# Forming the last product of a decoder block from seven quarter products instead of eight, with the sums of the weights' quarters kept in DRAM

## The chip, the cores and the metric

The kernel runs on one core of a Trainium2 chip. The metric is device time in microseconds (us) of one execution. Runs of the kernel before took 837.92 us (median of 3, 837.61 to 838.16).

Names used below: TensorE (PE) does the matmuls, and its weight loads (PEld) overlap them; VectorE (DVE) and GpSimd (POOL) do elementwise work, ScalarE (ACT) casts and activations; SyncE (SP) issues the DMA transfers, one after the other in the order written. PSUM has eight banks of 128 x 512 floats, in which the matmuls accumulate.

## The reference

A decoder block with 512 tokens, width 1024 and one layer: two token mixers side by side, merged by gates, then a SwiGLU channel mixer and a final norm. The change touches the last two lines:

```python
h = rmsnorm(x, norm1_g); z = h @ w_in + b_in
...
x = x + m @ w_mix_out
h = rmsnorm(x, norm2_g)
x = x + (silu(h @ ffn_w1) * (h @ ffn_w3)) @ ffn_w2     # ffn width 2816 = 22 x 128
return rmsnorm(x, norm_f_g)
```

All is float32. The product with `ffn_w2` is 512 x 2816 times 2816 x 1024.

## The kernel before

Every large product is done in three terms. An operand `v` is split into `h`, a cast to TensorE's reduced float32 form, and `l = v - h`; a product is then `xh.wh + xh.wl + xl.wh`, three matmuls for each 128 x 128 by 128 x 512 block. The cast is made on ACT (line 108, `split_to`), the difference on the engine that the caller names (line 104, `sub`): POOL or DVE.

Weights stream through a list of chunks (`wchunk`, line 121). A chunk is loaded by SP into one of four raw tiles of 128 x 1024 (pool `raws`, 512 KB, line 128), then split into one of five tiles that hold both halves (pool `hls`, line 135). `weights(key)` (line 150) emits loads and splits up to four chunks beyond the one asked for. The tile framework orders the instructions of each engine and picks free buffers; each engine then works strictly in its order, and an instruction that waits holds up those behind it.

Long-lived tiles of 128 x 512 come from a pool of 69 (`longt`), short-lived ones from a pool of 5 (`shortt`). PSUM is a pool of six banks (`bank`) and one of two (`bank2`).

The parts that the change touches, in order of time:

- *Mixing product* (`mix_rows`, line 679). For each of four row tiles `t` of 128 tokens the residual `x2[t]` (two tiles of 128 x 512) gets the product added by DVE (line 683), is normed and kept in SBUF to the end of the kernel.
- *FFN stage, called f below* (lines 704 to 719). For each of the 22 chunks `j` of the FFN width, 48 matmuls make `p1` and `p3` (hidden x tokens, each 128 x 512) from the chunks `f1_j` and `f3_j`. `ffn_out` (line 698) applies silu on ACT, multiplies on DVE and splits the result into `g[j]`. The difference of a split is POOL's for `f1_j` and DVE's for `f3_j` (lines 216 and 217). Chunks go in the order 0, 1, 2, ...
- *Output stage, called o below* (lines 721 to 751). All eight PSUM banks hold the result, four row tiles by two halves. For each `k` of the 22 chunks of `ffn_w2`, 24 matmuls add to the banks; the last four `k` (`LAST`) are left to the end and done row tile by row tile. Behind each row tile stand the addition of the residual (line 737), squares on ACT with a running sum (lines 311 and 315), the root (line 316), its reciprocal (line 317), two scalings (lines 748 and 749) and two stores of 256 KB (line 751).

Of the kernel before, what the change touches and what calls it, by code (L numbers as in the profile page):

```python
# [25 lines left out]
NT = T // P  # L26
ND = D // P
NR = DR // P
NF = DF // P
# [46 lines left out]
def tile_block(ctx, tc, a, out):  # L76
    nc = tc.nc
    pool = lambda name, bufs, **k: ctx.enter_context(tc.tile_pool(name=name, bufs=bufs, **k))
    consts = pool("consts", 1)
    raws = pool("raws", RAW)  # L80
# [16 lines left out]

    def bank2(name):
        return psum2.tile([P, T], F32, tag="cv", name=name)

    vec, act, pe, pool_e = nc.vector, nc.scalar, nc.tensor, nc.gpsimd

    def sub(eng, o, x, y):
        eng.tensor_tensor(out=o, in0=x, in1=y, op=ALU.subtract)  # L104

    def split_to(h, l, full, eng, copy=act.copy):

        copy(h, full)  # L108
# [12 lines left out]
    def wchunk(key, src, kt, cols, where="hl", lo=pool_e, after=None):  # L121
        chunks.append((key, src, kt, cols, where, lo, after))
# [86 lines left out]
    LAST = 4  # L209
# [8 lines left out]
    w2 = a["ffn_w2"][0].rearrange("(k p) (o n) -> p k o n", p=P, o=1)  # L218
    for k in range(NF):
        wchunk(f"f2_{k}", w2[:, k, :, :], 1, D, lo=vec if k % 2 else pool_e)  # L220

# [7 lines left out]
    for name, n in ROWS:  # L229
# [4 lines left out]
        while done < n:  # L234
            m = min(n - done, P - row_at(at + done)[1])
# [70 lines left out]
    def rstd_of(halves, junk, between=None):  # L306

        i = n_stats[0]
        n_stats[0] += 1
        ss, r = stats[:, i, :2], stats[:, i, 2:3]  # L310
        act.activation(junk[0], halves[0], AF.Square, accum_out=ss[:, 0:1])
        vec.tensor_scalar(out=ss[:, 0:1], in0=ss[:, 0:1], scalar1=1.0 / D, scalar2=EPS, op0=ALU.mult, op1=ALU.add)
        if between:
            between()
        act.activation(junk[1], halves[1], AF.Square, accum_out=ss[:, 1:2])  # L315
        act.activation(r, ss[:, 1:2], AF.Sqrt, scale=1.0 / D, bias=ss[:, 0:1])
        vec.reciprocal(r, r)
        return r

    def turn_half(name, rows, gname, dest, hf, bk):  # L320

        cs = slice(hf * 256, hf * 256 + 256)
        for c in range(ND):
            ps = bk[c % len(bk)](f"{name}{hf}{c}")
            for t in range(2):
                src = rows[2 * hf + t][c // 4][:, (c % 4) * P : (c % 4 + 1) * P]
                pe.transpose(ps[:, t * P : (t + 1) * P], src, ident)  # L327
            g = pc(gname, c)
            h, l = (v[:, cs] for v in dest[c])
            act.activation(h, ps[:, :256], AF.Copy, scale=g)  # L330
            vec.scalar_tensor_tensor(out=l, in0=ps[:, :256], scalar=g, in1=h.bitcast(F32), op0=ALU.mult, op1=ALU.subtract)  # L331

    def parts_of(pair_tiles, cs=slice(0, T)):
        return [(h[:, cs], l[:, cs]) for h, l in pair_tiles]
# [9 lines left out]
    HALVES = [slice(0, 256), slice(256, 512)]  # L344
    EARLY = 2
# [42 lines left out]
    ab, e, s, s2, po, c4 = (sm[:, i, :] for i in range(6))  # L388
# [210 lines left out]
    y = []  # L599
# [28 lines left out]
    for j in range(8):  # L628
        ws = w_tiles(f"lo{j}_0", 5) + w_tiles(f"lo{j}_1", 5)
# [19 lines left out]
    def token_banks(name):  # L649
        return [[(bank if t < 3 else bank2)(f"{name}{t}{h}") for h in range(2)] for t in range(NT)]  # L650

    def token_mm(po_, n_k, k, x_, w_, t, h):
        xh, xl = (v[:, t * P : (t + 1) * P] for v in x_[k])
        wh, wl = w_[h]
        for i, (l_, r_) in enumerate(((xh, wh), (xh, wl), (xl, wh))):
            pe.matmul(po_[t][h], l_, r_, start=k == 0 and i == 0, stop=k == n_k - 1 and i == 2)  # L656
# [13 lines left out]
    for k in range(8 - LAST):  # L670
        w_ = w_halves(f"mx{k}")
# [21 lines left out]
    mix_rows(3)  # L693


    g = []

    def ffn_out(j, p1, p3):
        s_ = shortt(f"si{j}")
        act.activation(s_, p1, AF.Silu)  # L700
        vec.tensor_tensor(out=s_, in0=s_, in1=p3, op=ALU.mult)  # L701
        g.append(split(f"gg{j}", s_, vec))

    wf = [(w_tiles(f"f1_{j}", ND), w_tiles(f"f3_{j}", ND)) for j in range(EARLY)]
    pf = [(bank(f"f1_{j}"), bank(f"f3_{j}")) for j in range(EARLY)]
    for hf in range(2):
        if hf:
            turn_half("th", xs, "norm2_g", h2p, 1, [bank2])
        for j in range(EARLY):
            for w_, p_ in zip(wf[j], pf[j]):  # L710
                mm3(p_[:, HALVES[hf]], w_, parts_of(h2p, HALVES[hf]))
    h2 = parts_of(h2p)
    for j in range(EARLY):
        ffn_out(j, *pf[j])
    for j in range(EARLY, NF):
# [6 lines left out]
    for h in range(2):  # L722
        nc.sync.dma_start(gf[h], a["norm_f_g"][h * T : (h + 1) * T].partition_broadcast(P))
    po_ = token_banks("o")
    for k in range(NF - LAST):
        w_ = w_halves(f"f2_{k}")
        for t in range(NT):
            for h in range(2):
                token_mm(po_, NF, k, g, w_, t, h)
    wl_ = [w_halves(f"f2_{k}") for k in range(NF - LAST, NF)]  # L730
    o_nat = out.rearrange("b (t p) d -> p (b t) d", p=P)
    for t in range(NT):

        def sums(h):
            for i in range(LAST):
                token_mm(po_, NF, NF - LAST + i, g, wl_[i], t, h)
            vec.tensor_tensor(out=x2[t][h], in0=po_[t][h], in1=x2[t][h], op=ALU.add)  # L737

        o = [shortt(f"of{t}{h}") for h in range(2)]

        def between():
            vec.tensor_tensor(out=o[0], in0=x2[t][0], in1=gf[0], op=ALU.mult)
            sums(1)
            vec.tensor_tensor(out=o[1], in0=x2[t][1], in1=gf[1], op=ALU.mult)

        sums(0)
        r = rstd_of(x2[t], po_[t], between)
        vec.tensor_scalar(out=o[1], in0=o[1], scalar1=r, scalar2=None, op0=ALU.mult)
        act.activation(o[0], o[0], AF.Copy, scale=r)  # L749
        for h in (1, 0):  # L750
            nc.sync.dma_start(o_nat[:, t, h * T : (h + 1) * T], o[h])


# [31 lines left out]
```

## Time and profile before

The profiled execution took 838.9 us, of which 837.1 are the span from its first to its last instruction.

| what | value |
|---|---|
| median of 3 runs | 837.92 us |
| profiled execution, its span | 838.9 us, 837.1 us |
| mean granted TensorE clock | 0.996 |
| bytes moved by transfers | 87.03 MB |
| transfers issued by SP | 311 |
| matmuls of the output stage | 528 |

The page gives the busy time of every engine, the span in 40 slices, the chain of work that ended last, and the costliest groups of instructions. In a group's row, `out<-in` names the tiles, `x22` the count, then busy time, mean time of one in ns, and how long the engine sat idle before these instructions and for whom. In the rows of windows, the busy time of each engine in a stretch is followed by the granted clock, the mean busy share of the 16 DMA engines and GB/s.

### The profile page before, as it was taken

To read this page: it belongs to the slowest core of one execution; us is meant where nothing else is said; L and a number is where in the kernel's file an instruction comes from. 1 tells how busy PE (TensorE), PEld (TensorE's weight loads), DVE (VectorE), ACT (ScalarE), POOL (GpSimd) and SP (SyncE) were. 2 spreads that over 40 slices of the span, in tenths; PEclk is the share of its full clock that TensorE was granted. 3 is DMA by queue.
4 is the path that set the end of the run, shared out by engine and by line. 5 is a ranking of instruction groups with operands and counts; after the bars stand their busy time and mean duration, and the time that the engine had idled before them with its cause. 6 is when DMAs were issued, how large, how long until landed. Compare 5 with 4: busy or idle time off the path is not lost.

```text
span 837.1 us, 10129 instructions
## 1 busy us (share of the span) xinstructions
PE 826.4 (99%) x3840; PEld 691.7 (83%) x3840; DVE 477.9 (57%) x656; ACT 385.6 (46%) x532; POOL 294.3 (35%) x153
## 2 busy tenths in 40 slices
PE   7999999999999999999999999999999999999997
PEld 7988888888888888888888998888888888888885
DVE  4699999999999945804633354344433343211115
ACT  6545688678579555722243352222222222222214
POOL 3565446444535443455471022222221112222210
PEclk9999999999999999999999999999999999999999
DMA  6634434334323322353274033333333333322202
GB/s 203 164 105 111 113 100 123 99 103 111 100 82 104 107 79 66 91 152 126 101 230 122 1 101 101 101 91 89 98 100 101 101 100 108 115 88 94 76 1 100
DMA packets 134580, 87.03 MB, mean 104 GB/s; under 512 B 8727, under 2 KB 125891, under 8 KB 134531
## 3 DMA queue, kind: packets, MB, share of 16 engines
q1 hardware_dynamic: 134531, 86.39, 34.9%
q8 instruction: 30, 0.49, 0.2%
q14 instruction: 19, 0.16, 0.1%
HBM read 81.25 MB, written 2.10 MB: 100 GB/s over the span
## 4 chain that ended last, share of the span: by engine, by line
PE 98%; DMA 1%; ACT 0%; SPq 0%; issue 0%; DVE 0%
PE z L295 34%; PE f L295 29%; PE o L656 14%; PE yb L295 7%; PE mx L656 5%; PE ya L295 5%; PE g L566 3%; DMA raw_in<-in_w_in_dram 1%; PE th L327 0%; PE tx L327 0%; SPq L251 0%; ACT o L315 0%; ACT of L749 0%; DVE x L737 0%; SPq L244 0%
## 5 line engine op out<-in xcount | busy, mean ns | idle before, releaser
L108 ACT CAST hl_f<-raw_f 128x1024 fp32r<-128x1024 f32 x66 | 69.5, 1053 | 243.0 <-issue 155.5
L104 POOL TENSOR_TENSOR hl_f<-raw_f,hl_f 128x1024 fp32r<-128x1024 f32 x33 | 79.0, 2394 | 287.8 <-ACT hl_f L108 287.8
L104 POOL TENSOR_TENSOR hl_in<-raw_in,hl_in 128x1024 fp32r<-128x1024 f32 x52 | 125.4, 2416 | 137.3 <-ACT hl_in L108 132.6
L445 DVE SCALAR_TENSOR_TENSOR cv<-u,par,cv 128x511 f32<-128x511 f32 (+17 forms) x240 | 162.6, 729 | 1.4 <-ACT cv L442 1.2
L104 DVE TENSOR_TENSOR hl_f<-raw_f,hl_f 128x1024 fp32r<-128x1024 f32 x33 | 41.5, 1256 | 144.4 <-ACT hl_f L108 144.4
L108 ACT CAST hl_in<-raw_in 128x1024 fp32r<-128x1024 f32 x52 | 54.3, 1044 | 11.8 <-PE z L295 7.1
L701 DVE TENSOR_TENSOR si<-si,f 128x512 f32<-128x512 f32 x22 | 15.1, 688 | 63.5 <-PE f L295 62.8
L295 PE MATMUL z<-h10h,hl_in 128*128 128x512 f32 (+1 forms) x112 | 42.4, 380 | 1.7 <-DVE h10l L331 1.7
L295 PE MATMUL z<-h16h,hl_in 128*128 128x512 f32 (+1 forms) x112 | 42.0, 376 | 0.0
L295 PE MATMUL z<-h17h,hl_in 128*128 128x512 f32 (+1 forms) x112 | 42.0, 376 | 0.0
L295 PE MATMUL z<-h15h,hl_in 128*128 128x512 f32 (+1 forms) x112 | 41.9, 376 | 0.0
L295 PE MATMUL z<-h11h,hl_in 128*128 128x512 f32 (+1 forms) x112 | 41.8, 375 | 0.0
L295 PE MATMUL z<-h13h,hl_in 128*128 128x512 f32 (+1 forms) x112 | 41.8, 375 | 0.0
L295 PE MATMUL z<-h14h,hl_in 128*128 128x512 f32 (+1 forms) x112 | 41.8, 375 | 0.0
L295 PE MATMUL z<-h12h,hl_in 128*128 128x512 f32 (+1 forms) x112 | 41.8, 375 | 0.0
L104 POOL TENSOR_TENSOR hl_lo<-raw_lo,hl_lo 128x640 fp32r<-128x640 f32 x16 | 25.9, 1624 | 35.8 <-ACT hl_lo L108 35.8
L295 PE MATMUL f<-h22h,hl_f 128*128 128x512 f32 (+1 forms) x96 | 35.4, 371 | 0.0
L295 PE MATMUL f<-h25h,hl_f 128*128 128x512 f32 (+1 forms) x96 | 35.4, 372 | 0.0
L295 PE MATMUL f<-h23h,hl_f 128*128 128x512 f32 (+1 forms) x96 | 35.4, 372 | 0.0
L295 PE MATMUL f<-h24h,hl_f 128*128 128x512 f32 (+1 forms) x96 | 35.4, 372 | 0.0
L295 PE MATMUL f<-h26h,hl_f 128*128 128x512 f32 (+1 forms) x96 | 35.4, 371 | 0.0
L295 PE MATMUL f<-h20h,hl_f 128*128 128x512 f32 (+1 forms) x96 | 35.0, 373 | 0.3 <-ACT h20h L330 0.3
(594 smaller groups left out, 2201.1 us busy)
## 6 DMA issues: line engine op xcount, KB each, us to landing
raw_f<-in_ffn_w_dram SPq DMA_DIRECT2D x66, 512.0 KB
raw_in<-in_w_in_dram SPq DMA_DIRECT2D x52, 512.0 KB
raw_lo<-in_lru_w_out_dram SPq DMA_DIRECT2D x16, 320.0 KB
x<-in_x_dram SPq DMA_DIRECT2D x16, 256.0 KB
raw_co<-in_conv_w_out_dram SPq DMA_DIRECT2D x8, 512.0 KB
raw_mx<-in_w_mix_out_dram SPq DMA_DIRECT2D x8, 512.0 KB
out_dram<-of SPq DMA_DIRECT2D x8, 256.0 KB
gfh<-in_norm_f_g_dram SPq DMA_DIRECT2D x1, 256.0 KB
```

The lines of the kernel that those rows point to most:

```text
L104: eng.tensor_tensor(out=o, in0=x, in1=y, op=ALU.subtract)
L108: copy(h, full)
L295: pe.matmul(ps, l, r, start=i == 0, stop=i == n - 1)
L445: vec.scalar_tensor_tensor(out=acc[c][:, s:], in0=u[c][:, : T - s], scalar=dw(c, s), in1=acc[c][:, s:], op0=ALU.mult, op1=ALU.add)
L566: pe.matmul(ps, l, r, start=k == 0, stop=k == len(mms) - 1)
L656: pe.matmul(po_[t][h], l_, r_, start=k == 0 and i == 0, stop=k == n_k - 1 and i == 2)
L701: vec.tensor_tensor(out=s_, in0=s_, in1=p3, op=ALU.mult)
```

## The change

The output product is cut into quarters: tokens in two halves of 256, columns of `ffn_w2` in two halves of 512, and the FFN width in two halves of 11 chunks (`KH`). A block product of two by two quarters, usually eight products, is formed from seven, with sums and differences of quarters (the Strassen-Winograd scheme). It does the following:

- The FFN chunks go in the order 0, 11, 1, 12, ... (`PAIRED`). When a pair is complete, `pair_out` forms the sums of the quarters of the activations on DVE, and splits two of the operands; the rest stays unsplit (`e`, `va`).
- `weight_sums` then loads the two `ffn_w2` rows of the pair into two raw tiles, makes four sums of quarters `t1` to `t4` on DVE and stores them to DRAM, 256 KB each.
- The difference of the split of `f1_j` moves from POOL to DVE.
- The residual `x2` is stored to DRAM after the mixing product (eight stores), and loaded again in the first step of the output stage, together with the norm's gain.
- The output stage has three passes over `k` = 0 to 10. Pass A makes three products (banks `r1`, `r2`, `r5`) from quarters of `ffn_w2` and `t1`, pass B three (`r7`, `r1` again, and `r3` in variable `r2`) from `t2`, `t3` and `ffn_w2`, pass C one from `t4`, on top of `r1`. During pass A, the operands `e` and `va` are split for B and C. A chunk of weights is now two quarters, each a transfer of its own of 256 KB.
- Sums of products are formed by DVE between the passes. The first two row tiles are finished during pass C; for the last two the products of the last three `k` are held back and done in `finish`.

```diff
-    for j in range(NF):
-        wchunk(f"f1_{j}", w1[:, :, j * P : (j + 1) * P], ND, P)
+    KH = NF // 2
+    PAIRED = [j for k in range(KH) for j in (k, k + KH)]
+    for j in PAIRED:
+        wchunk(f"f1_{j}", w1[:, :, j * P : (j + 1) * P], ND, P, lo=vec)
         wchunk(f"f3_{j}", w3[:, :, j * P : (j + 1) * P], ND, P, lo=vec)
-    for k in range(NF):
-        wchunk(f"f2_{k}", w2[:, k, :, :], 1, D, lo=vec if k % 2 else pool_e)
+    def quarters(key, of):
+        def load(raw):
+            for i, q in enumerate(of):
+                nc.sync.dma_start(raw[:, i * T : (i + 1) * T], q)
+        wchunk(key, load, len(of), T, lo=vec)
+    for n, q, m in (("A", [b11, kept("t1")], b21), ("B", [kept("t2"), kept("t3")], b22)):
+        for k in range(KH):
+            if k % 2 == 0:
+                quarters(f"o{n}s{k}", two(m, k))
+            quarters(f"o{n}{k}", [v(k) for v in q])
+    for k in range(0, KH, 2):
+        quarters(f"oC{k}", two(kept("t4"), k))
...
+            nc.sync.dma_start(x2_kept[t][h][:, :], x2[t][h])
...
-        vec.tensor_tensor(out=s_, in0=s_, in1=p3, op=ALU.mult)
-        g.append(split(f"gg{j}", s_, vec))
+        for dst, cs in zip(uv[k], HALVES):
+            vec.tensor_tensor(out=dst[:, HALVES[i]], in0=s_[:, cs], in1=p3[:, cs], op=ALU.mult)
+        if i:
+            pair_out(k, *uv[k])
+            weight_sums(k)
+    def pair_out(k, ua, va):
+        u_ = split(f"ua{k}", ua, vec)
+        s1 = shortt(f"s1{k}")[:, LO]
+        add(s1, va[:, LO], va[:, HI])
+        sp = longt(f"s1p{k}", F32R)
+        split_to(sp[:, LO], sp[:, HI], s1, vec)
+        e = longt(f"ea{k}")
+        sub(vec, e[:, HI], ua[:, LO], va[:, LO])
+        sub(vec, va[:, LO], s1, ua[:, LO])
+        sub(vec, e[:, LO], ua[:, HI], va[:, LO])
+        ops.append((u_, sp, e, va))
+    def weight_sums(k):
+        q = [raws.tile([P, 1024], F32, tag="raw", name=f"ws{k}_{i}") for i in range(2)]
+        for i, v in enumerate(q):
+            nc.sync.dma_start(v, w2[:, k + KH * i, :])
+        (q11, q12), (q21, q22) = ((v[:, :T], v[:, T:]) for v in q)
+        sub(vec, q22, q22, q12)
+        sub(vec, q12, q12, q11)
+        add(q11, q22, q11)
+        sub(vec, q21, q21, q11)
+        for n, v in (("t1", q12), ("t2", q11), ("t3", q22), ("t4", q21)):
+            nc.sync.dma_start(sums_[n, k][:, :], v)
...
+    def product(banks, i, x_, w_, start, stop, again=False):
+        (xh, xl), (wh, wl) = x_, w_
+        ts = slice(i * P, (i + 1) * P)
+        for n, (l_, r_) in enumerate(((xh, wh), (xh, wl), (xl, wh))):
+            pe.matmul(banks[i], l_[:, ts], r_, start=start and n == 0, stop=stop and n == 2, skip_group_check=again)
...
+    r1, r2, r5 = ([bank(f"{n}{i}") for i in range(2)] for n in ("r1", "r2", "r5"))
+    for k in range(KH):
+        if k % 2 == 0:
+            m_ = pairs_of(f"oAs{k}")
+        wb11, wt1 = pairs_of(f"oA{k}")
+        u_, sp, e, va = ops[k]
+        a11, a12, s1 = quarter(u_, LO), quarter(u_, HI), (sp[:, LO], sp[:, HI])
+        todo = [(r1, a11, wb11), (r2, a12, m_[k % 2]), (r5, s1, wt1)]
+        ends = k == KH - 1
...
+        late.append((split(f"eb{k}", e, vec), split(f"vb{k}", va, vec)))
+        if k == 0:
+            for t in range(NT):
+                for h in range(2):
+                    nc.sync.dma_start(x2[t][h], x2_kept[t][h][:, :])
...
+        todo = [(r7, quarter(e, HI), wt3), (r1, quarter(va, LO), wt2), (r2, quarter(e, LO), m_[k % 2])]
...
+    for i in range(2):
+        add(x2[i][1], q[i], x2[i][1])
+        add(x2[2 + i][1], q[i], x2[2 + i][1])
+        add(x2[i][1], r2[i], x2[i][1])
+        for h in range(2):
+            add(x2[2 + i][h], r7[i], x2[2 + i][h])
...
+    HOLD = KH - 3
+    held_ = []
+    for k in range(KH):
+        if k % 2 == 0:
+            m_ = pairs_of(f"oC{k}")
+        args = (quarter(late[k][1], HI), m_[k % 2])
+        if k < HOLD:
+            for i in range(2):
+                product(r1, i, *args, False, False, True)
+        else:
+            held_.append(args)
+        if k < 2:
+            finish(k, 0)
+    for i in range(2):
+        def rest():
+            for n, args in enumerate(held_):
+                product(r1, i, *args, False, n == len(held_) - 1, True)
+            add(x2[2 + i][0], r1[i], x2[2 + i][0])
+        finish(2 + i, 1, rest)
```

`finish` is the old row tile's end: the square of one half, `rest`, the square of the other, the root, two scalings and two stores. SP issues 448 transfers in the changed kernel, 311 before.

More of the change, by code (lines that the diff above doesn't have):

```diff
@@ L693, in tile_block @@
     mix_rows(3)
-    g = []
+    add = lambda o, x, y: vec.tensor_tensor(out=o, in0=x, in1=y, op=ALU.add)
+    LO, HI = HALVES
+    ops = []
+    uv = []
     def ffn_out(j, p1, p3):
@@ L708, in tile_block @@
             turn_half("th", xs, "norm2_g", h2p, 1, [bank2])
-        for j in range(EARLY):
-            for w_, p_ in zip(wf[j], pf[j]):
+        for i in range(EARLY):
+            for w_, p_ in zip(wf[i], pf[i]):
                 mm3(p_[:, HALVES[hf]], w_, parts_of(h2p, HALVES[hf]))
     h2 = parts_of(h2p)
-    for j in range(EARLY):
-        ffn_out(j, *pf[j])
-    for j in range(EARLY, NF):
+    for i, j in enumerate(first_two):
+        ffn_out(j, *pf[i])
+    for j in PAIRED[EARLY:]:
         p1, p3 = bank(f"f1_{j}"), bank(f"f3_{j}")
@@ L719, in tile_block @@
         ffn_out(j, p1, p3)
-    gf = pairt("gf", F32)
[L722 to L727, printed above, removed]
-            for h in range(2):
[L729 to L739, printed above, removed]
-        def between():
[L742 to L751, printed above, removed]
@@ new lines, in product, with pairs_of @@
+    def product(banks, i, x_, w_, start, stop, again=False):
[3 more added lines that the diff above has]
+            pe.matmul(banks[i], l_[:, ts], r_, start=start and n == 0, stop=stop and n == 2, skip_group_check=again)
+    x2 = [[longt(f"x2b{t}{h}") for h in range(2)] for t in range(NT)]
+    gf = pairt("gf", F32)
+    o_nat = out.rearrange("b (t p) d -> p (b t) d", p=P)
+    late = []
+    def pairs_of(key):
+        h, l = weights(key)
+        return [(h[:, i, :], l[:, i, :]) for i in range(h.shape[1])]
@@ new lines, in quarter @@
+    def quarter(p_, cs):
+        return tuple(v[:, cs] for v in p_)
+    r1, r2, r5 = ([bank(f"{n}{i}") for i in range(2)] for n in ("r1", "r2", "r5"))
[7 more added lines that the diff above has]
+        ends = k == KH - 1
+        order = [(r, i) for i in range(2) for r in (0, 1)] + [(2, 0), (2, 1)] if ends else [(r, i) for r in range(3) for i in range(2)]
+        for r, i in order:
+            product(todo[r][0], i, *todo[r][1:], k == 0, ends)
+            if ends and r == 1:
+                for b_ in (r1, r2):
+                    add(x2[i][0], b_[i], x2[i][0])
+        late.append((split(f"eb{k}", e, vec), split(f"vb{k}", va, vec)))
[3 more added lines that the diff above has]
+                    nc.sync.dma_start(x2[t][h], x2_kept[t][h][:, :])
+            for h in range(2):
+                nc.sync.dma_start(gf[h], a["norm_f_g"][h * T : (h + 1) * T].partition_broadcast(P))
@@ new lines, in tile_block @@
+    r2, r7 = [bank(f"r3{i}") for i in range(2)], [bank2(f"r7{i}") for i in range(2)]
+    q = [longt(f"q{i}") for i in range(2)]
+    for i in range(2):
+        act.copy(q[i], r5[i])
+    for k in range(KH):
+        if k % 2 == 0:
+            m_ = pairs_of(f"oBs{k}")
+        wt2, wt3 = pairs_of(f"oB{k}")
+        e, va = late[k]
+        todo = [(r7, quarter(e, HI), wt3), (r1, quarter(va, LO), wt2), (r2, quarter(e, LO), m_[k % 2])]
+        ends = k == KH - 1
+        for r in (1, 2, 0) if ends else (0, 1, 2):
+            for i in range(2):
+                product(todo[r][0], i, *todo[r][1:], r != 1 and k == 0, ends, r == 1)
+                if ends and r == 1:
+                    add(q[i], r1[i], q[i])
@@ new lines, in tile_block, with finish, scaled @@
+    for i in range(2):
[4 more added lines that the diff above has]
+            add(x2[2 + i][h], r7[i], x2[2 + i][h])
+    def finish(t, h, rest=None):
+        o = [shortt(f"of{t}{i}") for i in range(2)]
+        def scaled(i):
+            vec.tensor_tensor(out=o[i], in0=x2[t][i], in1=gf[i], op=ALU.mult)
+        def between():
+            scaled(h)
+            if rest:
+                rest()
+            scaled(1 - h)
+        r = rstd_of([x2[t][h], x2[t][1 - h]], [bank(f"jk{t}{i}") for i in range(2)], between)
+        vec.tensor_scalar(out=o[1 - h], in0=o[1 - h], scalar1=r, scalar2=None, op0=ALU.mult)
+        act.activation(o[h], o[h], AF.Copy, scale=r)
+        for i in (1 - h, h):
+            nc.sync.dma_start(o_nat[:, t, i * T : (i + 1) * T], o[i])
@@ new lines, in tile_block @@
+    HOLD = KH - 3
+    held_ = []
+    for k in range(KH):
+        if k % 2 == 0:
+            m_ = pairs_of(f"oC{k}")
+        args = (quarter(late[k][1], HI), m_[k % 2])
+        if k < HOLD:
+            for i in range(2):
+                product(r1, i, *args, False, False, True)
[3 more added lines that the diff above has]
+            finish(k, 0)
+    for i in range(2):
+        def rest():
[3 more added lines that the diff above has]
+        finish(2 + i, 1, rest)
```

16 lines of the change are left out of this document (13 added, 3 removed).

## The prediction

> **What bounds the kernel now.** I read the page first (busy shares, then the chain that ended last), then the chain of waits over the last 140 us, then windows of the two FFN stages with their transfer rates, then groups by line on DVE, ACT and POOL, and last the timeline of the tail.
>
> ```profile
> span 837.1 us, 10129 instructions
> PE 826.4 (99%) x3840; PEld 691.7 (83%) x3840; DVE 477.9 (57%) x656; ACT 385.6 (46%) x532; POOL 294.3 (35%) x153
> PE 98%; DMA 1%; ACT 0%; SPq 0%; issue 0%; DVE 0%
> ```
>
> ```profile
> 699.93 11.33 PE f L295 x50
> 711.26 119.69 PE o L656 x528
> ...
> 830.98 0.70 DVE x L737
> ...
> 832.98 0.72 ACT of L749
> ```
>
> ```profile
> core 0: us, PE busy (x) PEld busy (x) DVE busy (x) ACT busy (x) POOL busy (x), PEclk, DMA share, GB/s
> 484.00:711.00 227.00, 227.00 (x1040) 189.53 (x1040) 94.01 (x67) 69.31 (x89) 50.30 (x21) 1.00 0.34 100
> 711.00:831.00 120.00, 119.94 (x530) 98.97 (x528) 26.15 (x36) 28.78 (x40) 21.51 (x9) 1.00 0.24 79
> 424.00:428.00 4.00, 4.00 (x19) 3.34 (x18) 0.69 (x1) 4.00 (x8) 2.90 (x3) 1.00 0.98 316
> 440.00:450.00 10.00, 10.00 (x46) 8.29 (x45) 2.50 (x4) 2.71 (x4) 3.38 (x2) 1.00 0.81 216
> ```
>
> TensorE is the bound: 98% of the chain is matmul, and from 484 to 831 it has no gap. In the output stage every wait that ends last is a matmul, and DVE, ACT and the transfers are busy a quarter of the time. There a matmul costs 119.69 / 528 = 0.2267 us from start to start, at full clock. So one matmul fewer is worth that much, as long as the weights still come in time. The profiled execution took 838.9 us around a span of 837.1 and lies 0.98 above the median of the runs, 837.92.
>
> **What is removed.** The output product, 22 x 24 = 528 matmuls, becomes 7 products x 11 steps x 2 row tiles x 3 terms = 462, with the same shapes. 66 x 0.2267 = 14.96 us leave the path. All else must hide behind TensorE, or is paid.
>
> **FFN stage (f).** Durations from groups by line, windows 484 to 711 (f) and 711 to 838 (o):
>
> ```profile
> L104 DVE TENSOR_TENSOR hl_f<-raw_f,hl_f 128x1024 fp32r<-128x1024 f32 x22 | 26.9, 1224 | 50.9 <-ACT hl_f L108 50.9
> L701 DVE TENSOR_TENSOR si<-si,f 128x512 f32<-128x512 f32 x21 | 14.4, 688 | 60.4 <-PE f L295 59.7 <-ACT si L700 0.7
> L104 DVE TENSOR_TENSOR gg20l<-si,gg20h 128x512 fp32r<-128x512 f32 x1 | 2.5, 2468 | 0.9 <-ACT gg20h L108 0.9
> L331 DVE SCALAR_TENSOR_TENSOR h26l<-th,par,h26h 128x256 fp32r<-128x256 f32 x1 | 0.5, 485 | 0.6 <-ACT h26h L330 0.6
> L108 ACT CAST hl_f<-raw_f 128x1024 fp32r<-128x1024 f32 x43 | 45.3, 1052 | 153.5 <-issue 147.8 <-PE f L295 5.7
> L700 ACT ACTIVATE si<-f 128x512 f32<-128x512 f32 x22 | 12.9, 589 | 0.0
> L108 ACT CAST gg2h<-si 128x512 fp32r<-128x512 f32 x1 | 0.6, 613 | 0.0
> L749 ACT ACTIVATE of<-of,stats 128x512 f32<-128x512 f32 x4 | 2.9, 719 | 0.7 <-DVE stats L317 0.7
> ```
>
> A pair of chunks keeps TensorE for 96 x 0.2267 = 21.76 us. DVE per pair: four weight splits (two of them POOL's until now) 4 x 1.22 = 4.9; nine 256-wide operations at 0.45 each (no such row; between half of 0.69 and the 0.485 of the scalar form) 4.1; one 512-wide split 0.69; four sums of weight quarters 4 x 0.69 = 2.8. That is 12.4 of 21.76, with both bounds of the 256-wide price 11.5 to 12.7. The 2.47 us that a 512-wide split took beside a POOL split falls to 0.69 where POOL is idle. ACT keeps 4 x 1.05 + 2 x 0.59 + 0.61 + about 0.4 = 6.4. Transfers: 2.1 MB of f1/f3, 1.05 MB of w2 read and 1.05 MB of sums stored, 4.19 MB in 21.76 us = 193 GB/s. The trace has moved 316 at a share of 0.98 and 216 at 0.81 (267 if full), so the queue is 61 to 72% full. No row shows stores to DRAM under load; I price them as loads, and the lower end is in the range below.
>
> The waits are the risk: SP's queue is in order, and in it a load of a later chunk stands behind the four stores of sums, which wait for DVE, which waits for the w2 loads and for the end of a matmul group. Counted from the end of a group: the second w2 load goes out about 8 us after it, when the fourth split of the pair is done; DVE reaches the sums at 11 to 16 us, since it first waits for the next group to end, and the last load held up goes out at about 19. It is wanted in the ring of five split chunks at 27 at the earliest, as there a slot comes free only then, and by TensorE later still. So 8 us of raw slack, and one group, 10.9 us, more ahead of TensorE. Price 0; if the cover went, each us of lateness beyond some 19 would be paid in each of 11 pairs.
>
> **Entering pass A.** The first four chunks are split before f ends. With E the end of f (711.26 here): the fifth (step 2) waits for the last f slot, is cast and split by E+2.8 and wanted at E+8.2. The banks of the third product wait for DVE's multiplies after the last group, done by E+1.2, wanted at E+2.7. Price 0.
>
> The kept residual comes back in the same SP queue: ten transfers of 256 KB behind the chunks of step 5.
>
> ```profile
> 708.63 0.43 SPq L723 DMA_DIRECT2D gfh<-in_norm_f_g_dram  x1
> 421.11 4.03 SPq L668 DMA_DIRECT2D x<-in_x_dram  x8
> 427.67 20.41 SPq L133 DMA_DIRECT2D raw_f<-in_ffn_w_dram  x9
> 433.32 1.05 ACT L108 CAST hl_f<-raw_f 128x1024 fp32r<-128x1024 f32 x1 [4.65 <-PE mx L656]
> ```
>
> Issue is 10 x 0.43 = 4.3 us, data 2.6 MB at 316 = 8.3 us. The trace holds the like case: eight x loads, then weights, the first cast 433.32 - 427.67 = 5.65 us after its issue, an upper bound of landing behind 2 MB. The x loads start near E+3.6, the next weights (step 6) land near E+15 to 16.5; they are wanted by TensorE at E+24.5. Price 0, slack some 4 us after cast and split.
>
> **Steady passes.** One step of A or B is 18 matmuls, 4.08 us, and 1.5 chunks in three loads of 256 KB: again 193 GB/s, and 1.3 us of issue. In A, DVE does 1.5 x 1.22 + 2 x 0.69 for the operands of the later passes = 3.2, with gaps 3.4; ACT 1.5 x 1.05 + 2 x 0.61 = 2.8. Both below 4.08, DVE at 83%. But they are in order: a cast waits for a ring slot, and the operand splits queue behind it. Walking the order through, DVE has the last operand split at about E+38, seven before pass A ends at E+44.9, and each chunk is ready 3 to 5 us ahead; the first of pass B, the tightest, at E+42. In B DVE drops to 1.9 of 4.08. Price 0, at most a few us (a rival below).
>
> The Trainium skill, in DMA: Bandwidth & Descriptors (sections Anatomy of one DMA and Rules for kernel authors), speaks against this change: it fits a fixed 2.0 us plus bytes / 436e3 to each transfer, mostly the receipt, heaviest to HBM, and wants 1 MiB or more per transfer. By it a 256 KB quarter takes 2.6 us, and 77 of them, one after another, 200 us instead of 105. The window 424 to 428, in which the eight 256 KB transfers of x land, speaks against that: 316 GB/s, so the fixed part overlaps.
>
> **Pass C and the tail.** C has 66 matmuls, 14.96 us, and DVE must combine the seven products, split three chunks and scale two row tiles. From its first addition, 3.4 us before C, to the split of the last quarter there are 12 additions, 3 chunk splits, 3 multiplies, a scaling, 3 small operations and that split.
>
> ```profile
> 817.38 0.69 DVE L737 TENSOR_TENSOR x<-o,x 128x512 f32<-128x512 f32 x1 [1.30 <-PE o L656]
> 817.99 0.15 DVE L317 RECIPROCAL stats<-stats 128x1 f32<-128x1 f32 x1
> 831.70 0.60 ACT L315 ACTIVATE o<-x 128x512 f32<-128x512 f32 x1 [2.00 <-DVE x L737]
> 832.24 0.19 ACT L315 ACTIVATION_READ_ACCUMULATOR o<-x 128x1 f32 x1
> 832.46 0.29 ACT L316 ACTIVATE stats<-stats 128x1 f32<-128x1 f32 x1
> ```
>
> Where nothing is waited for, the next operation starts 0.61 after a 0.69 one; as dependent ones 0.73. That makes 13.9 to 16.6 us, done 10.5 to 13.2 after C starts; TensorE wants it after 55 matmuls, 12.5. So 0 to 0.7 us of gap, I take 0.3, nearer the independent spacing.
>
> After its last matmul the old kernel takes 833.70 - 830.98 = 2.72 us to the last scaling and 3.4 more to the end. Now two row tiles end together: one more scaling on ACT (0.72) stands between the last square and its root, and an addition's worth of DVE work beside it; two more stores go out just ahead of the last two. Bounds 0 and 0.72 + 0.73 + 0.8 = 2.3; I take 1.1.
>
> **Sum.** 838.9 - 14.96 + 0.3 + 1.1 = 825.3 for a profiled execution; less 0.98, 824.4 us for the median. Own range 822.9 (the matmuls alone) to 826.5.
>
> **Rivals.**
> *C and the tail are dearer*: DVE, in order, is late for the held products and the last additions by both upper bounds and a chunk split more: 822.96 + 0.7 + 2.3 + 1.2 = 827.2, up to 829. For: the queue there is full for 13 us. Against: only one split has no slack.
> *Pass A loses steps to its ring*: slack of 3 to 5 us after the reload and at the first chunk of B is used up once or twice, 4 to 8 us: 828 to 832. For: in-order queues, five slots, one chunk held two steps. Against: DVE 83%.
> *Slower: pass A goes serial.* If a chunk's cast and split and the operand casts and splits follow each other instead of overlapping, a step costs 1.5 x (1.05 + 1.22) + 2 x (0.61 + 0.69) = 6.0 instead of 4.08, 11 x 1.9 = 21 us: 824.4 + 21 = 845. It decides once the step exceeds 4.08; beyond about 5.3 the change loses. For: ACT and DVE wait for each other in each split. Against: four raw tiles and five split ones let them overlap.
> *Slower by transfers*, the rule named above: quarters or stores move at less than the 193 GB/s needed, on which both stages depend. At 150 the 11 pairs and the passes take 28% longer, over 344 us about +96: some 920. For: no stores under load in the trace. Against: 216 to 316 GB/s in it.
> *It doesn't save what it says*: excluded by the count, unless a matmul of it is dearer; operands have the old shapes.
>
> **Chances.** Forecast 0.70; dearer C and tail 0.09; A loses steps 0.11; serial A 0.06; transfers 0.04. Within 0.2% (836.2 to 839.6, about what a measurement of this kernel can tell from no change) lies the thin end between the third and fourth, 0.02; slower 0.10; faster 0.88. The range 822.6 to 831 holds the first two and most of the third.
>
> **What would show it.** Right: matmuls of the output stage without gaps, 462 x 0.2267 = 104.7 us from E to the last; f unchanged at E near 711; DVE near 12.4 us per pair; transfers near 190 GB/s at a share of 0.6 to 0.7 from 485 on; 2.7 to 5 us from the last matmul to the last scaling. Wrong: TensorE waiting for a split chunk in f or A, gaps at the first chunk of B, or SP waiting for stores while the ring runs dry.

## The result, and the profile after

| | before | changed |
|---|---|---|
| median (lowest to highest), 4 runs each | 837.76 us (836.98 to 838.16) | 824.15 us (823.17 to 824.76) |
| profiled execution, its span | 838.9 us, 837.1 us | 823.95 us, 821.4 us |
| bytes moved by transfers | 87.03 MB | 122.96 MB |

The ratio is 0.9838, with a 95% interval of 0.982 to 0.9855: 13.6 us less, where 824.4 us had been forecast. The page of the changed kernel, its first lines and its chain by engine:

```profile
span 821.4 us, 10487 instructions
PE 810.8 (99%) x3774; PEld 678.1 (83%) x3774; DVE 556.5 (68%) x849; ACT 412.3 (50%) x574; POOL 215.4 (26%) x120
...
PE 97%; ACT 1%; DMA 1%; DVE 1%; issue 0%; SPq 0%; ACTq 0%
```

TensorE is still the bound: 66 matmuls fewer, all else busier, and the chain is matmul to 97%. The chain of waits from 690 us on:

```profile
689.86 19.95 PE f L319 x88
709.81 102.69 PE r L794 x453
...
812.53 0.70 DVE x2b L727
...
814.57 0.70 DVE x2b L727
...
817.04 0.72 ACT of L869
```

E, the start of the output stage, lies at 709.81. The piece of 453 matmuls runs from there without a gap (102.69 / 453 = 0.2267 each), and nine more for the last row tile follow while DVE and ACT already finish the row tile before it. From E to the last addition, which waits for the last matmul, it is 104.8 us; 462 x 0.2267 = 104.7 was forecast. The table of TensorE's waits confirms it: after the start of f it has none, in f or in a pass.

```profile
engine line waited for: us in total, times, longest us
PE f L319 <- ACT h20h L354: 0.3, 1, 0.3
```

The windows of f, of passes A, B and C, and of two stretches in the entry to A (after the clock come the transfers' share and GB/s):

```profile
484.00:709.81 225.81, 225.81 (x1029) 188.41 (x1029) 120.76 (x190) 65.79 (x86) 0.00 (x0) 1.00 0.65 198
709.81:754.70 44.89, 44.89 (x199) 37.17 (x199) 37.05 (x50) 29.94 (x42) 0.00 (x0) 1.00 0.75 246
754.70:799.60 44.90, 44.90 (x199) 37.18 (x199) 23.21 (x24) 18.70 (x21) 0.00 (x0) 1.00 0.62 192
799.60:814.50 14.90, 14.90 (x66) 12.01 (x64) 13.46 (x25) 8.61 (x20) 0.00 (x0) 1.00 0.19 70
...
716.00:722.00 6.00, 6.00 (x28) 4.99 (x27) 3.72 (x4) 2.63 (x3) 0.00 (x0) 1.00 1.05 346
722.00:728.00 6.00, 6.00 (x28) 4.96 (x27) 4.59 (x6) 4.71 (x7) 0.00 (x0) 1.00 1.03 367
```

In every row TensorE's busy time equals the length of the window, at full clock. DVE took 120.76 / 225.81 x 21.76 = 11.6 us per pair of chunks in f (12.4 forecast), and 37.05 / 11 = 3.37 us per step of A (3.2, with gaps 3.4). Where the residual comes back, the last two rows, the queue is full for 12 us, and TensorE has no gap there either.

**The two spans add up.** They differ by 15.7 us. Of this, 14.96 are the matmuls. The tail gives back 0.7: from the last addition to the end of the last scaling it is 817.76 - 814.57 = 3.19 us instead of 2.72, and from there to the end 3.64 instead of 3.4. The other 1.45 belong to no part of the change. The first long stretch of matmuls at the kernel's start, in the chain of before and then of the changed kernel:

```profile
28.54 44.19 PE z L295 x240
```

```profile
27.04 44.19 PE z L319 x240
```

It began 1.5 us earlier in the execution profiled after; from its start to E there are 682.72 us before and 682.77 after. So f costs TensorE what it did, and the lead comes from the start, which was late in the one execution profiled before: e1_old_less64 below, the same kernel as before up to E, began this stretch at 26.89 and had E at 709.62.

### The profile page after: what moved, and what is told of

The parts are those of the page before. It is cut to its first block, busy times and chain, and to the rows that moved or that the text cites. A ratio compares the mean times of both kernels' runs of the same rounds, so it can differ in the third digit from the quotient of the medians.

```text
span 821.4 us, 10487 instructions
## 1 busy us (share of the span) xinstructions
PE 810.8 (99%) x3774; PEld 678.1 (83%) x3774; DVE 556.5 (68%) x849; ACT 412.3 (50%) x574; POOL 215.4 (26%) x120
## 2 busy tenths in 40 slices
DMA packets 154310, 122.96 MB, mean 150 GB/s; under 512 B 10919, under 2 KB 128083, under 8 KB 154259
## 4 chain that ended last, share of the span: by engine, by line
PE 97%; ACT 1%; DMA 1%; DVE 1%; issue 0%; SPq 0%; ACTq 0%
PE z L319 34%; PE f L319 29%; PE r L794 13%; PE yb L319 7%; PE mx L680 5%; PE ya L319 5%; PE g L590 3%; DMA raw_in<-in_w_in_dram 1%; PE th L351 0%; PE tx L351 0%; DVE x L366 0%; SPq L275 0%; DVE x2b L727 0%; DVE of L859 0%; ACT hl_in L108 0%
## 5 line engine op out<-in xcount | busy, mean ns | idle before, releaser
L108 ACT CAST hl_f<-raw_f 128x1024 fp32r<-128x1024 f32 x44 | 46.3, 1053 | 149.3 <-PE f L319 83.1
L104 DVE TENSOR_TENSOR hl_f<-raw_f,hl_f 128x1024 fp32r<-128x1024 f32 x44 | 53.8, 1222 | 49.2 <-ACT hl_f L108 49.2
L739 DVE TENSOR_TENSOR ua<-si,f 128x256 f32<-128x256 f32 x22 | 9.3, 422 | 62.9 <-PE f L319 62.2
L319 PE MATMUL f<-h27h,hl_f 128*128 128x512 f32 (+1 forms) x96 | 35.3, 371 | 0.0
L319 PE MATMUL f<-h21h,hl_f 128*128 128x512 f32 (+1 forms) x96 | 35.3, 371 | 0.0
```

Source lines behind the costliest of these rows:

```text
L319: pe.matmul(ps, l, r, start=i == 0, stop=i == n - 1)
L739: vec.tensor_tensor(out=dst[:, HALVES[i]], in0=s_[:, cs], in1=p3[:, cs], op=ALU.mult)
```

## The experiments

Intervals are those of the ratio to the kernel before, run on the same chip in the same stretch. Its medians there were 837.95 (with the first four), 837.59 (next four) and 837.62 (last four).

| run | median (lowest to highest), us | 95% interval |
|---|---|---|
| e1_old_less64 | 822.93 (822.48 to 823.65) | 0.9807 to 0.9836 |
| e2_f1_pool | 823.54 (822.67 to 824.03) | 0.9812 to 0.9841 |
| e3_hold5 | 823.15 (822.88 to 823.97) | 0.9809 to 0.9842 |
| e4_two_terms | 805.43 (804.04 to 806.17) | 0.9595 to 0.9624 |
| e5_ring4 | 823.85 (823.81 to 824.11) | 0.9819 to 0.9848 |
| e6_stores2 | 823.41 (822.68 to 824.83) | 0.9815 to 0.9844 |
| e6_stores3 | 826.04 (824.96 to 827.13) | 0.9844 to 0.9874 |
| e7_reload2 | 825.02 (823.83 to 825.23) | 0.9826 to 0.9858 |
| e8_after_again (the changed kernel) | 824.29 (822.91 to 824.92) | 0.9821 to 0.9852 |
| e9_hold5_again | 823.07 (822.67 to 823.38) | 0.981 to 0.9837 |
| e10_stores3_late | 823.64 (822.92 to 824.66) | 0.9819 to 0.9849 |
| e11_stores3_again | 825.6 (824.88 to 827.82) | 0.9844 to 0.9874 |

### Is the gain the matmuls alone? e1_old_less64

The kernel before, with 64 of its 528 output matmuls left out: the third term (`xl.wh`) of the first eight `k`.

```diff
         for i, (l_, r_) in enumerate(((xh, wh), (xh, wl), (xl, wh))):
+            if n_k == NF and k < 8 and i == 2:
+                continue
```

> The kernel before with 64 matmuls fewer: in the output stage the third term (low half of the activations) is left out for the first 8 of 22 steps; nothing else differs. Theory (a matmul is worth its spacing of 0.2267 us and nothing but TensorE sets the time): 64 x 0.2267 = 14.5 us less, 823.3 where the kernel before takes 837.8, and the changed kernel (66 fewer, with all its extra work) lies within 1 us of it. Rival (the changed kernel gains something beside its matmuls, from the idle POOL or the early sums, and pays part of it back): this kernel saves clearly more or less than 14.5.

Measured 822.93, 15.0 us below the kernel before it. This kernel has no sums of quarters, no stores, no reload and no passes, and two matmuls more than the changed one; the changed kernel is 1.2 us behind it, a little more than the 1 us expected. By the profiles it should be 0.25 behind: 0.7 of tail (above) less two matmuls, 0.45. The rest is no more than the spread of one kernel's runs. So all that forms and feeds the seven products costs 0.7 us by the profiles, and 1.7 at most by the medians (1.2 and the two matmuls). Its chain:

```profile
709.62 105.19 PE o L658 x464
```

105.19 / 464 = 0.2267: the matmuls' spacing is the same in both kernels.

### Does the split moved off POOL matter? e2_f1_pool

```diff
-        wchunk(f"f1_{j}", w1[:, :, j * P : (j + 1) * P], ND, P, lo=vec)
+        wchunk(f"f1_{j}", w1[:, :, j * P : (j + 1) * P], ND, P)
```

> The changed kernel with the difference of the f1 splits on POOL again. Theory (f is bound by TensorE, DVE has 9 us of 21.76 per pair to spare, and the splits are ready a group ahead): the same time, 824.2 within 0.7, though 512-wide DVE operations beside a POOL split take 2.4 us again. Rival (the move to DVE was needed, since the DVE operations of the sums are held up by POOL): f grows by some tenths of a us per pair, 2 to 10 us in all, 826 to 834.

Measured 823.54, within the spread of the changed kernel. The piece of 453 matmuls is again 102.69 us long. One of the four sums of a pair took DVE 2.16 us on average instead of 0.69, as expected beside POOL, and f had no gap. The move neither costs nor brings anything that these runs can tell: both engines have room.

### Is there slack behind the cover? e4_two_terms

If TensorE's work hides everything, taking a third of it away shows how much sooner the rest could have been done. The output products are formed from `xh.wh` and `xl.wl` alone. Both cross terms, `xh.wl` and `xl.wh`, are left out, so this is not the full product: 308 matmuls instead of 462, while all loads, casts, splits and sums stay.

```diff
-        for n, (l_, r_) in enumerate(((xh, wh), (xh, wl), (xl, wh))):
+        for n, (l_, r_) in enumerate(((xh, wh), (xl, wl))):
```

> The changed kernel with two matmuls instead of three for each block of the output stage (high x high, low x low; the cross terms are left out): 308 matmuls, a step of 12 takes TensorE 2.72 us, with all loads and splits as they were. It shows the next bound. If TensorE alone set the time: 154 x 0.2267 = 34.9 us less than the changed kernel, 789. Theory (DVE with 3.4 us per step in pass A is next): pass A 37 us instead of 30, pass B bound by TensorE, pass C late by 3 to 6 us, 798 to 804. Rival (cast, split and operand splits follow each other, 6.0 us per step): pass A 66 us, 825 to 832. Rival (transfers: 768 KB per step at 267 to 316 GB/s): 2.5 to 2.9 us per step, 789 to 796.

(All four tiles of a block are still read.) Measured 805.43, 1.4 us above the expected range. The windows of its three passes, and of the stretch around one gap of TensorE:

```profile
709.95:745.60 35.65, 32.73 (x136) 25.95 (x134) 29.85 (x40) 25.56 (x36) 0.00 (x0) 0.95 0.85 292
745.60:782.00 36.40, 32.13 (x130) 25.05 (x130) 27.47 (x30) 21.82 (x27) 0.00 (x0) 0.95 0.76 248
782.00:797.00 15.00, 12.11 (x44) 9.27 (x44) 15.00 (x29) 8.32 (x19) 0.00 (x0) 0.89 0.23 85
...
729.00:730.00 1.00, 0.00 (x0) 0.00 (x0) 0.00 (x0) 0.65 (x1) 0.00 (x0) 1.00 1.08 408
...
731.00:732.00 1.00, 0.94 (x4) 0.48 (x3) 1.00 (x2) 1.00 (x2) 0.00 (x0) 1.00 0.54 205
732.00:733.00 1.00, 1.00 (x4) 0.76 (x4) 1.00 (x2) 1.00 (x2) 0.00 (x0) 0.59 0.28 66
733.00:734.00 1.00, 1.00 (x3) 0.76 (x3) 1.00 (x3) 1.00 (x3) 0.00 (x0) 0.50 0.79 272
734.00:735.00 1.00, 1.00 (x4) 0.76 (x3) 1.00 (x1) 1.00 (x2) 0.00 (x0) 0.50 0.77 240
735.00:736.00 1.00, 1.00 (x5) 0.83 (x4) 1.00 (x3) 0.95 (x2) 0.00 (x0) 0.70 0.59 219
736.00:737.00 1.00, 1.00 (x6) 0.82 (x5) 1.00 (x2) 0.78 (x2) 0.00 (x0) 1.00 0.64 195
```

Two thirds of the matmuls would take 29.9, 29.9 and 10.0 us, 69.8 in all; the passes took 87.05. TensorE stood idle for some 10 of that (its busy times add to 76.97), and the lowered clock accounts for some 5 more: 0.05 x 35.65 + 0.05 x 36.40 + 0.11 x 15.00 = 5.3. The last 2 are not accounted for. The theory's one bound, DVE, is not what was met in A and B: there DVE was busy 84% and 75%. Its chain in B shows a loop instead:

```profile
763.00 1.06 ACT hl_oB L108
...
764.09 1.24 DVE hl_oB L104
...
765.34 0.32 SPq L232
...
765.70 4.37 DMA raw_oB<-t
...
770.17 1.06 ACT hl_oB L108
```

A raw tile is cast, split and only then loaded again, 7.17 us a round; in it, four raw tiles bring four chunks. That is 2.69 us for the 1.5 chunks of a step, about TensorE's own 2.72, so the loop alone does not make B's 36.4 us. Waits of 1.6 us at its start, a lowered clock (1.7 us) and 2.7 us at its end, in which TensorE already waits for DVE ahead of C, make most of the excess. In C, DVE is busy all the time. For the changed kernel this gives the margin that the prediction had to guess: supply can be had at 35.65 / 11 = 3.24 us a step in A and 36.4 / 11 = 3.31 in B, lowered clock included, where three terms need 4.08. The serial step of 6.0 us, the rival by which the change would have lost, is excluded by this run too.

### How much ring does it need? e5_ring4

```diff
-HL = 5
-AHEAD = 4
+HL = 4
+AHEAD = 3
```

> The changed kernel with four split tiles instead of five, and three chunks ahead instead of four. Theory (pass A has 3 to 5 us of slack at each chunk): a slot freed at the end of a step is wanted again one step, 4.08 us, later, and cast and split take 2.3 us plus what queues ahead of them, so it just fits or loses a us now and then: 824 to 829. Rival (the fifth tile is what keeps pass A from going serial): one to two us per step in A, and in the other stages too, 835 or more.

Measured 823.85, no loss: the chain again holds the stage's matmuls in one piece (102.96 us for 454). The fifth slot isn't needed, and the rival in which pass A loses steps to its ring has no ground.

### What do the stores cost? e6_stores2 and e6_stores3

Each of the 44 sums is stored twice, then three times (`range(2)` below), the copies to places that nobody reads.

```diff
             nc.sync.dma_start(sums_[n, k][:, :], v)
+            for c in range(1):
+                nc.sync.dma_start(more_[n, k, c][:, :], v)
```

> The changed kernel with each sum of weight quarters stored twice, to two places in DRAM: 5.24 MB per pair instead of 4.19, 241 GB/s instead of 193. Theory (transfers cost nothing until the queue is full, stores like loads): the same time, 824.2 within 0.7, DMA share 0.75 to 0.9 in f. Rival (stores to DRAM are dearer than loads, and the queue is near full): f grows, by 11 x 1 to 3 us, 835 to 857.

> The same with each sum stored three times: 6.29 MB per pair, 289 GB/s over 21.76 us, between the 267 and the 316 GB/s that full windows of the trace before give. Theory: at 316 still hidden, 824; at 267 a pair takes 23.6 us, 11 x 1.8 = 20 us more, 844. Whichever end it is nearer to is the price of stores that the prediction had open.

Twice: 823.41, no cost. Three times: 826.04, some 1.9 above the changed kernel. But f itself did not lengthen: its window, and two of the entry to A, in e6_stores3:

```profile
484.00:709.00 225.00, 225.00 (x1032) 187.88 (x1031) 123.60 (x193) 68.02 (x89) 0.00 (x0) 1.00 0.89 291
...
722.00:728.00 6.00, 6.00 (x28) 4.86 (x27) 3.35 (x6) 3.31 (x5) 0.00 (x0) 1.00 1.04 384
728.00:734.00 6.00, 4.38 (x18) 3.03 (x17) 4.68 (x6) 4.42 (x7) 0.00 (x0) 1.00 0.62 214
```

At 291 GB/s, half as much again as the 198 of the changed kernel, f shows no gap. The gap comes at 728, behind the residual. The chain there:

```profile
715.67 0.38 SPq L830
...
716.15 6.00 DMA x2b<-x2k
...
722.16 7.10 DMA raw_oA<-t
```

SP issues the residual (L830 in this kernel), its transfers take 6 us, and the weights behind them 7.1. TensorE waits 1.2 and 0.5 us for two split chunks, together about the whole loss.

### Is it the reload's place? e10_stores3_late, beside e8_after_again and e11_stores3_again

Sums stored three times, and the residual loaded in the sixth step of A instead of the first:

```diff
-        if k == 0:
+        if k == 5:
             for t in range(NT):
                 for h in range(2):
                     nc.sync.dma_start(x2[t][h], x2_kept[t][h][:, :])
```

> The changed kernel as it is, for a comparison side by side with the three that follow. 824.2 us, as in its first runs (823.2 to 824.8).

> Every sum stored three times, the residual loaded after step 0, beside the former. Theory and rival: 826.0, some 1.8 us above the changed kernel, with TensorE waits of 1 to 2 us for split chunks some 18 to 20 us after the end of f.

> Every sum of the weights' quarters is stored three times, as in an earlier run that took 826.0, but the kept residual is loaded after step 5 of pass A instead of step 0. Theory (the extra stores cost nothing in f, and the loss comes only from the residual's loads standing ahead of the weights of step 6 while the queue still works off the stores): the TensorE waits at the entry of pass A go, and the time is that of the changed kernel beside it within 0.5 us, 824.2. Rival (the loss is the stores' own backlog at the end of f, and would delay any load behind them): still 825.5 to 826.5, with waits at steps 2 to 6 of pass A.

With the reload at its old place 825.6, TensorE waiting 1.2 and 0.5 us for split chunks, as in the first such run. With the late reload 823.64, no wait of TensorE in the passes, and the time of the changed kernel beside it (824.29) but for 0.65 us, which the spread covers. The runs of the two places do not overlap. A window of e10 over the late reload:

```profile
734.00:740.00 6.00, 6.00 (x29) 4.95 (x28) 5.64 (x8) 4.89 (x9) 0.00 (x0) 1.00 1.04 389
```

The transfers are at a full share there too, and TensorE has no gap. So the loss is not the price of the stores themselves. It comes from the reload's place, where it falls on a queue that still works off f, and that is a place at which the changed kernel could lose time to transfers.

### How near is that place in the changed kernel? e7_reload2

The residual is loaded twice in the first step, 2 MB more in the same queue.

```diff
-            for t in range(NT):
-                for h in range(2):
-                    nc.sync.dma_start(x2[t][h], x2_kept[t][h][:, :])
+            for _ in range(2):
+                for t in range(NT):
+                    for h in range(2):
+                        nc.sync.dma_start(x2[t][h], x2_kept[t][h][:, :])
```

> The changed kernel with the kept residual loaded twice in the first step of pass A, sixteen transfers instead of eight, ahead of the weights of step 6 in SP's queue. Theory (about 4 us of slack after the reload): 2.1 MB more at 316 GB/s is 6.6 us, so the weights of step 6 are late by 0 to 3 us: 824 to 827. Rival (the queue behind the reload has more room than reckoned): the same time within 0.7. Rival (pass A was already losing steps there): the whole 6.6 us, 831.

Measured 825.02, up to 0.9 above the changed kernel, but its profile has no gap of TensorE (the piece of 453 matmuls takes 102.69 us), and the runs of the two overlap. The second load is 2.1 MB, and at the 357 to 391 GB/s of the windows from 722 to 734 it holds the queue for 5 to 6 us more.

That is more than the slack. Of the two chunks of step 6, the one split last, with the first matmuls that read it, in the changed kernel and then in e7 (the x3 row belongs to the other chunk):

```profile
729.20 1.23 DVE L104 TENSOR_TENSOR hl_oA<-raw_oA,hl_oA 128x1024 fp32r<-128x1024 f32 x1 [0.33 <-ACT hl_oA L108]
...
734.13 0.62 PE L794 MATMUL r<-hl_oA,ua6h 128*128 128x512 f32 x2
```

```profile
735.24 0.84 PE L794 MATMUL r<-hl_oAs,ua6h 128*128 128x512 f32 x3
...
735.61 1.22 DVE L104 TENSOR_TENSOR hl_oA<-raw_oA,hl_oA 128x1024 fp32r<-128x1024 f32 x1
...
736.14 0.62 PE L794 MATMUL r<-hl_oA,ua6h 128*128 128x512 f32 x2
```

The changed kernel has this chunk split at 730.43, 3.7 us before its first matmul: the "some 4 us" of the prediction. In e7 it is split at 736.83, 1.6 us after the step has begun. There is no gap because in this kernel the order of the step's matmuls is another one: the chunk that was ready at 735.10 goes first. So the slack was used up, and the new order hid the rest.

### Is the tail what the prediction said? e3_hold5 and e9_hold5_again

The products of the last five `k`, not three, are held back for the last two row tiles, so that more matmuls lie between the ends of the two.

```diff
-    HOLD = KH - 3
+    HOLD = KH - 5
```

> The changed kernel with the last five steps of pass C held back instead of three, so that row tile 2 gets its sum 15 matmuls (3.4 us) ahead of the last one instead of 9 (2.0 us). Theory (the tail is longer than before by the scalings of row tile 2 between the last square and its root): from the last matmul to the last scaling 2.7 us instead of 3.2, the whole 0.5 us shorter, 823.7. The last quarter is needed 6 matmuls (1.4 us) earlier; its split has 2 us of slack, so no gap. Rival (DVE's order in pass C has no room): a gap ahead of the held products of 0.5 us or more, and no gain.

> The products of the last five instead of three k are held back for the last two row tiles. Theory: 0.45 us less than the changed kernel beside it, as the profile showed the last row tile's last addition to last scaling at 2.73 instead of 3.19 us. Rival: no difference beyond 0.1 us, as the earlier profile's shorter tail was one execution's.

ACT's work after the last addition, in the timeline of the changed kernel (start, duration, instruction, and the idle time before it):

```profile
815.29 0.60 ACT L339 ACTIVATE jk<-x2b 128x512 f32<-128x512 f32 x1 [0.52 <-DVE x2b L727]
...
815.92 0.71 ACT L869 ACTIVATE of<-of,stats 128x512 f32<-128x512 f32 x1
816.53 0.28 ACT L340 ACTIVATE stats<-stats 128x1 f32<-128x1 f32 x1
```

and in e9_hold5_again:

```profile
815.51 0.60 ACT L339 ACTIVATE jk<-x2b 128x512 f32<-128x512 f32 x1 [0.92 <-DVE x2b L727]
...
816.26 0.29 ACT L340 ACTIVATE stats<-stats 128x1 f32<-128x1 f32 x1
```

In the first, the scaling of the third row tile (L869) stands between the last square and its root, 1.24 us apart; in the second that scaling was over by 814.6, and they are 0.75 apart. From the last addition to the end of the last scaling it takes 3.19 us in the one and 2.73 in both profiles of the other, 2.72 in the kernel before. The times agree in sign, 823.07 against 824.29 beside it and 823.15 in the first run; the shorter tail explains 0.46 of that, and the rest lies within the spread (822.67 to 823.97 in eight runs, against 822.91 to 824.92). This is the best version found with the full product: half a microsecond by the profiles.

## Why the prediction was right

**What bounds, and what is removed.** Confirmed as put: 104.8 us from E to the last addition, the spacing of 0.2267 in e1 and in the changed kernel, and no gap.

**FFN stage at price 0.** Confirmed: 682.77 us from the first long stretch to E, 682.72 before. DVE's 12.4 us per pair became 11.6, near the lower bound of 11.5: the 256-wide operation, for which there was no row, takes 0.42 us instead of the assumed 0.45, and operations that do not depend on each other overlap a little, which a sum of durations leaves out.

```profile
L739 DVE TENSOR_TENSOR ua<-si,f 128x256 f32<-128x256 f32 x22 | 9.3, 422 | 62.9 <-PE f L319 62.2
```

The order was right in time too. One pair of chunks on DVE and in SP's queue:

```profile
601.12 0.42 DVE L739 TENSOR_TENSOR ua<-si,f 128x256 f32<-128x256 f32 x1 [3.16 <-PE f L319]
...
612.67 0.68 DVE L104 TENSOR_TENSOR ws<-ws,ws 128x512 f32<-128x512 f32 x1
```

```profile
615.12 1.77 SPq L767 DMA_DIRECT2D t<-ws  x3
620.01 2.32 SPq L133 DMA_DIRECT2D raw_f<-in_ffn_w_dram  x3
```

The group ends at about 601; the sums start 11.6 us after it (11 to 16 forecast) and the last load held up goes out at 19 (19 forecast). The stores under load, for which there was no row either, could be priced as loads: three times their number left f without a gap, as e6_stores3 showed.

**Entering pass A at price 0.** Right in price and in slack, a little off in time. The weights of step 6 were to land at E + 15 to 16.5; the casts of their two chunks, which waited for the transfer, began at 725.95 and 728.11, E + 16.1 and E + 18.3. So the first came as forecast and the second some 2 us later, though the queue moved 346 to 367 GB/s, not 316. The slack after cast and split was still 3.7 us, where some 4 had been reckoned; e7 used it up. e6_stores3 and e10 showed the mechanism that was feared, at its place, only not at this kernel's load.

**Steady passes at price 0.** The last operand split was due at E + 38, and ended at 746.6, E + 36.8; the first chunk of B was due at E + 42 and wanted at E + 44.9. It was split by 751.6, E + 41.8:

```profile
750.37 1.22 DVE L104 TENSOR_TENSOR hl_oB<-raw_oB,hl_oB 128x1024 fp32r<-128x1024 f32 x1 [1.49 <-ACT hl_oB L108]
```

The rivals here were answered by e4 (3.24 us a step could be had) and e5 (one slot less costs nothing). The rival of the transfers fell with the windows: 192 to 246 GB/s in the passes. The Trainium skill's figure in DMA: Bandwidth & Descriptors (Anatomy of one DMA), 2.0 us and bytes / 436e3 for each transfer, is a fit to transfers issued from GpSimd, while those here are SP's; the prediction used it without that condition. Taken all the same, it gives an estimate of 200 us for the 77 quarters one after another. A 256 KB transfer every 2.6 us would be 101 GB/s, and the windows in the entry to A moved 346 and 367: the transfers overlap, so that a fixed part, whatever its size, costs latency and not throughput. No run here shows its size.

**Pass C and the tail: two terms mis-sized.** The gap in C was put at 0.3, between 0 and 0.7. It is 0. DVE's list before the split of the last quarter, first and last row:

```profile
796.40 0.68 DVE L727 TENSOR_TENSOR q<-r,q 128x512 f32<-128x512 f32 x1
...
809.40 0.67 DVE L104 TENSOR_TENSOR hl_oC<-raw_oC,hl_oC 128x512 fp32r<-128x512 f32 x1
```

That is 13.7 us for exactly the operations listed, done 10.5 after C begins. The lower bound, 13.9, in which every operation follows the one before it as an independent one, was the right one, and the slack is 2 us. The tail, put at 1.1, measured 0.7: 0.47 for the one scaling between square and root, as described, and 0.24 for the stores. The addition's worth of DVE work beside it had no part in it.

**The sum.** The forecast took 0.98 us off the profiled time to come to the median. The step was right: the execution profiled before reached its first long stretch 1.5 us later than the one profiled after, which lies within 0.2 of its own median. The 0.3 and 0.4 too much in C and in the tail are smaller than the spread of one kernel's runs, 1.6 us. With these two terms as measured the sum would have been 823.7, 0.5 below the 824.15 that was measured; that 824.4 came within 0.3 of it is luck, as far as the tenths go. What held is the mechanism: the matmuls' count, their spacing, and the other work hidden behind them.

## What to carry to other kernels

Where one engine has no gap, the price of fewer of its instructions is their count times their spacing, and the work goes into showing that every other list (each engine in order, each queue) is done before it is wanted; these lists can be walked with durations of a few rows to within a microsecond or two. Look for the place where a burst of loads falls into an in-order queue that is already full: the FFN stage here bore three times the stores, and the same burst five steps later cost nothing. When two profiled executions are compared, first subtract what differs ahead of the change.

## What the hardware showed that was not expected

**Transfers.** The limit taken from the kernel before was 316 GB/s. In the reload, with 256 KB transfers, windows of 6 us moved 346 to 389 GB/s at shares of 1.03 to 1.05, and in e6_stores3 f sustained 291 GB/s of mixed loads and stores for 225 us at a share of 0.89.

**The clock after a short gap.** In e4, TensorE waited 2.2 us for a split chunk (`hl_oA`, 728.2 to 730.4). In the windows shown above the granted clock was still 1.00 until 732, then 0.59, 0.50, 0.50 and 0.70 for a microsecond each, and 1.00 again: 0.41 + 0.50 + 0.50 + 0.30 = 1.7 us lost on top of the 2.2. e4 shows two more such falls, behind waits of 0.66, 0.54 and 1.06 us within 4.2 us at the entry to B, and behind one of 3.6 us at the entry to C. Read from the clock of windows of 0.5 and 1 us, each of the three lasted 3.4 us at 0.50, and they began at about 732.2, 749.25 and 783.4, that is 17.1 and 34.1 us apart, five and ten times 3.41. It looks as if the clock could change only at fixed steps of 3.41 us, by how idle the step before had been; three falls of one execution do not prove it. In e11 gaps of 0.5 and 1.2 us were followed by windows at 1.00, and what decides between such cases is not shown. The Trainium skill, in TensorE: Matmul & The Clock Gate (Part 1: The HAM clock gate), puts the fall to half rate behind an idle window of about 3.4 us. The half rate agrees with the trace; two of the three falls here came behind shorter waits. The some 5 us that e4 lost in this way are more than the 1.4 by which it came out above its range, and a gap like that of 2.2 us in the passes of the changed kernel could have cost nearly twice its length.
